# Up panels of a gated FFN in pairs with seven-product units, and convolution taps on ScalarE

## The chip, the cores and the metric

The kernel runs on one core of one Trainium2 chip. The metric is device time in microseconds (us). The profile is one execution of the program, taken by the hardware profiler. PE is TensorE (matmuls), PEld its weight loads, DVE is VectorE, ACT is ScalarE, POOL is GpSimd, SP is SyncE; the q behind an engine's name is its queue for DMA issues.

## The reference

A decoder trunk of two layers on 256 tokens with a width of 2048, all in float32: a gated linear attention layer (GLA), then a forgetting attention layer (FoX), each with a cross attention into 256 memory tokens and a channel mixer, which is what the change touches. Each mixer (here: FFN) is a gated MLP with a causal convolution of width 3 along the tokens between the up projection and the gate. In short:

```
a, val = split(rmsnorm(x) @ w_up)                      # two halves of 5632 columns
a   = a[t]*g2 + a[t-1]*g1 + a[t-2]*g0 + bias            # each column has its own g and bias
val = val[t]*g2 + val[t-1]*g1 + val[t-2]*g0 + bias
x   = x + (silu(a) * val) @ w_down
```

## The kernel before, in words

**Products.** All matmuls of the projections run on float32 split in a high and a low part. A weight unit is a tile [128, 1024] of 512 KB (two chunks of 128 rows of the contraction, 512 columns each). It is loaded by SP into a ring of five (`raw`), cast by ACT to its high part (`whi`, ring of four, line 210), and DVE subtracts to get the low part (`wlo`, ring of four, line 219). Three matmuls then make one product of a token block of 128 with one chunk: x high by w high (L231), x low by w high (L232), x high by w low (L235). For two token blocks and two chunks that is 12 matmuls of 128x512 a unit.

**The FFN.** The hidden width of 5632 is 44 chunks of 128, in three parts: chunks 0 to 15, 16 to 31, 32 to 43 (`PARTS`). For each part the up panels run first, then the down projection of these chunks, which adds to the residual x. An up panel makes two chunks of both halves a and val, 512 columns in all, from 8 units; parts 1, 2 and 3 have 8, 8 and 6 panels. The very first two panels of a layer run interleaved (`proj_two`), all others one by one (`proj_tm`).

**After a panel.** ACT evacuates each token block with the norm's scale (L1118), DVE transposes 32x32 blocks (L440), ACT's DMA queue writes the tile to DRAM (`turned`, L443) and reads it back in four pieces (L448), so that features lie on partitions and tokens along the free axis (`u`, two tiles in turn, two zero columns ahead). The convolution follows in two steps of one chunk each (`taken`): per chunk and half one ACT Identity with bias and scale (L1094) and two DVE scalar_tensor_tensor (L1095, L1096); then Silu on ACT (L1098), the product on DVE (L1099) and a split in high and low part (L525 on ACT, L526 on DVE) as the input of the down projection.

**Order.** `later(units, step)` puts a step behind the cast of that many units after the panel's end: write at 3, reads at 6, the two convolution steps at 8 and 9. Casts and low halves are placed ahead of their use with a priority. Each engine runs its own list in order, so an instruction that waits holds back all that stand behind it on that engine.

**Seven products.** In the down projection of parts 1 and 2 two output panels run as a pair (`proj_seven`). For chosen units (3 and 5, or 3, 5 and 7) a 2x2 block product of (two token blocks) by (two panels, two chunks) is made from seven instead of eight products, 21 matmuls in place of 24. It needs sums of the activations (`token_sums`, the `forms` tiles), and sums of the two raw weight tiles on DVE (t13 and t24, L348 to L351, four subtractions of 128x512), whose high and low parts are then made as usual (L316, L317, the single one as vhi and vlo). Extra accumulators m1, m5, m6 and m7 lie in the banks ps_t, ps_o and ps_s. A variant, `seven_evacuated`, sums these four into three SBUF tiles (L382 to L386) and adds the result at the evacuation with a DVE scalar_tensor_tensor (L483 in its one place so far, in the FoX layer's projections).

Of the kernel before, what the change touches and what calls it, by code (L numbers as in the profile page):

```python
# [31 lines left out]
PARTS = ((0, 16), (16, 32), (32, 44))  # L32
# [5 lines left out]
NUNIT = 1024  # L38
AHEAD = 300
SEVEN = ((3, 5), (3, 5, 7))  # L40
LAST = ()

SPREAD = [128 * q + 32 * k + i for k in range(4) for i in range(32) for q in range(4)]

# [95 lines left out]
def _trunk(ctx: ExitStack, tc: tile.TileContext, xt, xtok, memt, wp, wgu, gns, gfin, cnv, par, msk, out):  # L140
    nc = tc.nc
    where, _ = _layout()
# [37 lines left out]
    def later(*steps):  # L180

        for units, step in steps:
            due.append([units, step])
# [72 lines left out]
    def proj_two(keys, src, evacs, late):  # L256

        units = [where[k] for k in keys]
        base = min(min(u[1]) for u in units[0])
        acc = [[pacc.tile([P, 512], F32, name="acc", tag="acc") for _ in range(2)] for _ in keys]  # L260
        count = len(units[0])
        for part in (range(count - late), range(count - late, count)):
            for i in range(2):
                for u in part:
                    unit = units[i][u]
                    hi, lo = split_unit(unit)
                    products(list(enumerate(acc[i])), src, base, unit, hi, lo, u == 0, u == count - 1)
# [106 lines left out]
    def seven_evacuated(keys, src, forms, evacs, tiles):  # L374

        n = where[keys[0]][0][2]
        extra = {}

        def more(m1, m5, m6, m7):
            u, v, w = (tiles(t, F32)[:, :n] for t in ("s16", "s165", "s1675"))  # L380
            m1, m5, m6, m7 = (m[:, :n] for m in (m1, m5, m6, m7))
            S.activation(u, m1, AF.Copy)  # L382
            V.tensor_tensor(u, u, m6, ALU.add)
            V.tensor_tensor(v, u, m5, ALU.add)
            V.tensor_tensor(u, u, m7, ALU.add)
            V.tensor_tensor(w, u, m5, ALU.add)  # L386
            extra.update({(0, 0): m1, (1, 0): v, (0, 1): u, (1, 1): w})

        def evac(i):
            return lambda b, a: evacs[i](b, a, extra[i, b])  # L390

        proj_seven(keys, src, forms, [evac(i) for i in range(2)], tiles, more, True)

    def sums_of(src, chunks, f, h, form):
# [56 lines left out]
    def back():  # L451
        return tp.tile([P, 4, T], F32, name="back", tag="back", bufs=2)
# [65 lines left out]
    def split(dst, i, src, g=None, dealt=True):  # L518

        hi, lo = dst[i][:, 0, :], dst[i][:, 1, :]  # L520
        if dealt:
            hi, lo = (v.rearrange("p (h t) -> p h t", h=2) for v in (hi, lo))
            src = src.rearrange("p (t h) -> p h t", h=2)
        if g is None:
            S.activation(hi, src, AF.Copy)  # L525
            V.tensor_tensor(lo, src, hi.bitcast(F32), ALU.subtract)  # L526
        else:
            S.activation(hi, src, AF.Copy, scale=g)
            V.scalar_tensor_tensor(lo, src, g, hi.bitcast(F32), ALU.mult, ALU.subtract)  # L529
# [535 lines left out]
    def ffn(l, nx, h, m, then, ending=None):  # L1065
        with tc.tile_pool(name=f"ffn{l}", bufs=1) as fp, ExitStack() as ends:
            if ending:
                then = ending[0](ends)
            sums = ends.enter_context(ExitStack())
            sp = sums.enter_context(tc.tile_pool(name=f"sums{l}", bufs=1))  # L1070
            cw = fp.tile([P, 4 * 88], F32, name="cw")
            nc.sync.dma_start(cw, cnv[l])
            us = [fp.tile([P, 4, T + 2], F32, name=f"u{i}") for i in range(2)]
            for u in us:
                nc.gpsimd.memset(u[:, :, :2], 0.0)
            turn = [0]
            tiles = [sp.tile([P, 2, 4, P], F32R, name=f"forms{i}") for i in range(3)]
            held = []

            def spare_tile(name, dtype):  # L1080
                return sp.tile([P, 512 if name in ("vhi", "vlo") else NUNIT], dtype, name=name, tag=name)

            def form(t):
                return lambda i: [t[:, h, i, :] for h in range(2)]

            def taken(j, base, u, i):

                cv = []
                for c in range(2):
                    v = u[:, 2 * c + i, :]  # L1090
                    col = (c * 44 + j + i) * 4
                    w = [cw[:, col + n : col + n + 1] for n in range(4)]
                    r = fp.tile([P, T], F32, name=f"cv{c}", tag=f"cv{c}", bufs=3)
                    S.activation(r, v[:, 2:], AF.Identity, bias=w[3], scale=w[2])  # L1094
                    V.scalar_tensor_tensor(r, v[:, 1 : T + 1], w[1], r, ALU.mult, ALU.add)  # L1095
                    V.scalar_tensor_tensor(r, v[:, :T], w[0], r, ALU.mult, ALU.add)  # L1096
                    cv.append(r)
                S.activation(cv[0], cv[0], AF.Silu)  # L1098
                V.tensor_tensor(cv[1], cv[0], cv[1], ALU.mult)  # L1099
                split(m, j + i - base, cv[1])  # L1100
                if (j - base) // 2 in parts[base]:
                    held.append(cv[1])
                    if i:
                        summed(parts[base][(j - base) // 2])

            def summed(form):
                ab = [natural(h)[:, :, b] for h in held for b in range(2)]
                held.clear()
                token_sums(*ab, sp.tile([P, 4, P], F32, name="sf", tag="sf"), [form[:, h, :, :] for h in range(2)])

            def panel(j, base, slack=0):
                held = []

                def evac(b, a):
                    if not held:
                        held.append(Turn("turned"))
                    e = tp.tile([P, 512], F32, name="scaled", tag="scaled", bufs=2)
                    S.activation(e, a, AF.Copy, scale=nx.col()[:, b : b + 1])  # L1118
                    held[0].put(b, e)
                    if not b:  # L1120
                        return
                    u = us[turn[0] % 2]
                    turn[0] += 1
                    later((3, held[0].write), (6, lambda: held[0].read(lambda k: u[:, k, 2:])),
                          (8 + slack, lambda: taken(j, base, u, 0)), (9 + slack, lambda: taken(j, base, u, 1)))

                return evac

            parts = {lo: dict(zip(SEVEN[1] if p < len(PARTS) - 1 else LAST, tiles)) for p, (lo, _) in enumerate(PARTS)}
            for p, (lo, hi) in enumerate(PARTS):  # L1130
                forms = parts[lo]
                js = list(range(lo, hi, 2))
                if not p:
                    proj_two([("up", l, j) for j in js[:2]], h, [panel(js[0], lo), panel(js[1], lo, 2)], 2)
                    js = js[2:]
# [177 lines left out]
```

## Time and profile before

| what | value |
|---|---|
| median of 3 runs | 2239.39 us (2239.23 to 2240.11) |
| the profiled execution | 2239.32 us |
| its span, first to last instruction | 2237.6 us |
| mean granted TensorE clock | 0.999 |
| PE busy | 2225.4 us, 99% of the span |
| DVE busy | 1654.5 us, 74% |
| ACT busy | 1293.9 us, 58% |
| mean DMA rate | 231 GB/s |

Busy time leaves out register, branch, semaphore and DMA-issuing instructions. Durations of matmuls are latencies: they overlap, so a matmul's price is the time of a stretch divided by its count. Rows of the groups have line, engine, operation, output and input names, shapes, count, then busy us and mean ns, then idle time of the engine ahead of them and what ended it. The first layer's FFN spans 466.8 to 1179.2 us (up panels of the second part 725 to 899.2, its down panels to 983.2), the second layer's from 1515.5 us.

### The profile page before, as it was taken

The page shows a single profiled execution, that of the slowest core. Times are in us where ns is not written, and L with a number is a line of the kernel's source. Part 1 is how long each engine was busy: PE and PEld are TensorE (multiplying, and loading weights), DVE is VectorE, ACT ScalarE, POOL GpSimd, SP SyncE. Part 2 cuts the span into 40 slices and gives each one's busy share as a digit, 9 for nine tenths or more (in the row PEclk, how much of TensorE's full clock was granted, in tenths as well). Part 3 has the DMA queues.
Part 4 walks back from the last instruction along what each step waited for, and adds up shares of the span by engine and source line. Part 5 has one row for each costly group of instructions (what it writes and reads, how often), then busy time and mean ns, then how long its engine had stood idle before and what let it go on. Part 6 is the DMA issues. An engine that isn't in the chain of part 4 may idle for free.

```text
span 2237.6 us, 29679 instructions
## 1 busy us (share of the span) xinstructions
PE 2225.4 (99%) x10267; PEld 1862.4 (83%) x10267; DVE 1654.5 (74%) x2608; ACT 1293.9 (58%) x1921; POOL 44.7 (2%) x71
## 2 busy tenths in 40 slices
PE   9999999999999999999999999999999999999998
PEld 7888888888888888888888898888888888888886
DVE  8568987667689676886767875666778867797766
ACT  7555666556565565555656555455656556555554
POOL 0000000000000000000000000000000000000000
PEclk9999999999999999999999999999999999999999
DMA  9875667678766777667778777677877678766774
GB/s 340 277 233 188 211 201 227 192 251 247 244 226 207 236 236 242 216 209 242 232 255 276 236 231 229 196 236 246 249 240 235 199 235 243 236 214 217 237 236 140
DMA packets 276894, 516.98 MB, mean 231 GB/s; under 512 B 149884, under 2 KB 158600, under 8 KB 276616
## 3 DMA queue, kind: packets, MB, share of 16 engines
q1 hardware_dynamic: 124296, 427.24, 58.9%
q10 hardware_dynamic: 149760, 80.51, 12.5%
q0 software_dynamic: 2688, 7.34, 1.1%
q8 instruction: 80, 1.31, 0.2%
q14 instruction: 70, 0.57, 0.1%
HBM read 470.44 MB, written 44.58 MB: 230 GB/s over the span
## 4 chain that ended last, share of the span: by engine, by line
PE 99%; DMA 1%; DVE 0%; ACT 0%; SPq 0%; issue 0%; DVEq 0%; ACTq 0%
PE acc L232 26%; PE acc L231 26%; PE acc L235 26%; PE acc L293 16%; PE ps_s L293 1%; PE ps_o L293 1%; PE ps_t L293 1%; DMA back<-turned 0%; PE ps_s L835 0%; PE ps_t L625 0%; PE ps_s L636 0%; PE ps_o L647 0%; DMA raw<-wp 0%; PE ps_s L1008 0%; PE ps_o L855 0%; PE ps_o L1024 0%
## 5 line engine op out<-in xcount | busy, mean ns | idle before, releaser
L219 DVE TENSOR_TENSOR wlo<-raw,whi 128x1024 fp32r<-128x1024 f32 (+4 forms) x763 | 908.7, 1198 | 434.0 <-ACT whi L210 407.4
L210 ACT ACTIVATE whi<-raw 128x1024 fp32r<-128x1024 f32 (+4 forms) x763 | 785.4, 1038 | 622.6 <-PE acc L232 295.3
L231 PE MATMUL acc<-whi,B 128*128 128x512 f32 (+3 forms) x1440 | 548.3, 383 | 0.0
L232 PE MATMUL acc<-whi,B 128*128 128x512 f32 (+3 forms) x1440 | 547.9, 382 | 0.0
L231 PE MATMUL acc<-whi,A 128*128 128x512 f32 x1120 | 435.9, 392 | 0.7 <-ACT whi L210 0.5
L232 PE MATMUL acc<-whi,A 128*128 128x512 f32 x1120 | 435.0, 390 | 0.0
L235 PE MATMUL acc<-wlo,B 128*128 128x512 f32 (+3 forms) x1440 | 376.2, 381 | 0.0
L231 PEld LDWEIGHTS acc<-whi,B 128*128 128x128 f32 x1440 | 270.4, 188 | 46.7
L232 PEld LDWEIGHTS acc<-whi,B 128*128 128x128 f32 x1440 | 270.1, 188 | 46.3
L235 PEld LDWEIGHTS acc<-wlo,B 128*128 128x128 f32 x1440 | 267.9, 188 | 46.1
L235 PE MATMUL acc<-wlo,A 128*128 128x512 f32 x1120 | 301.5, 390 | 0.0
L231 PEld LDWEIGHTS acc<-whi,A 128*128 128x128 f32 x1120 | 210.3, 188 | 45.2 <-ACT whi L210 1.1
L232 PEld LDWEIGHTS acc<-whi,A 128*128 128x128 f32 x1120 | 210.3, 188 | 43.6 <-DVE A L529 0.2
L235 PEld LDWEIGHTS acc<-wlo,A 128*128 128x128 f32 x1120 | 210.2, 188 | 43.8 <-DVE wlo L219 0.3
L293 PE MATMUL acc<-whi,B 128*128 128x512 f32 x508 | 132.8, 390 | 0.0
L293 PE MATMUL acc<-whi,A 128*128 128x512 f32 x496 | 130.7, 390 | 0.0
L1094 ACT ACTIVATE cv<-u,cw 128x256 f32<-128x256 f32 x176 | 99.7, 593 | 40.9 <-DMA u<-turned 40.7
L293 PEld LDWEIGHTS acc<-whi,B 128*128 128x128 f32 x508 | 95.2, 188 | 19.9
L293 PEld LDWEIGHTS acc<-whi,A 128*128 128x128 f32 x496 | 93.2, 188 | 19.7
L1095 DVE SCALAR_TENSOR_TENSOR cv<-u,cw,cv 128x256 f32<-128x256 f32 x176 | 79.9, 480 | 18.7 <-ACT cv L1094 18.5
L440 DVE STREAM_TRANSPOSE square<-scaled 128x512 f32<-128x512 f32 x122 | 80.0, 690 | 0.0
L1096 DVE SCALAR_TENSOR_TENSOR cv<-u,cw,cv 128x256 f32<-128x256 f32 x176 | 77.7, 479 | 0.0
(260 smaller groups left out, 1797.3 us busy)
## 6 DMA issues: line engine op xcount, KB each, us to landing
raw<-wp SPq DMA_DIRECT2D x743, 512.0 KB, 4.4
turned<-square ACTq DMA_DIRECT2D x61, 512.0 KB, 5.1
u<-turned ACTq DMA_DIRECT2D x176, 128.0 KB, 4.2
raw<-wp SPq DMA_DIRECT2D x32, 384.0 KB, 3.3
raw<-wp SPq DMA_DIRECT2D x24, 388.0 KB, 4.6
xturned<-square ACTq DMA_DIRECT2D x12, 512.0 KB, 4.3
back<-xturned ACTq DMA_DIRECT2D x40, 128.0 KB, 4.3
raw<-wp SPq DMA_DIRECT2D x8, 400.0 KB, 3.5
```

The source lines that it names most:

```text
L210: casts.append(S.activation(hi[:, s], raw[:, s], AF.Copy))
L219: V.tensor_tensor(lo[:, s], raw[:, s], hi[:, s].bitcast(F32), ALU.subtract)
L231: TE.matmul(acc[:, :n], xh, hi[:, s], start=first and j == 0, stop=False)
L232: TE.matmul(acc[:, :n], xl, hi[:, s], start=False, stop=False)
L235: TE.matmul(a, xh, ls, start=False, stop=stop)
L293: TE.matmul(a[:, :n], x, w, start=k not in begun, stop=calls[k] == 0)
L440: V.transpose(self.square[:, :, :, b], src.rearrange("p (c t) -> p c t", t=32))
L1094: S.activation(r, v[:, 2:], AF.Identity, bias=w[3], scale=w[2])
L1095: V.scalar_tensor_tensor(r, v[:, 1 : T + 1], w[1], r, ALU.mult, ALU.add)
L1096: V.scalar_tensor_tensor(r, v[:, :T], w[0], r, ALU.mult, ALU.add)
```

## The change

Panels of a part now run in pairs through `seven_evacuated` as long as more than two panels are left in the part, and units 3 and 5 of each pair (`UP`) use seven products. Part 1 keeps its first `proj_two`, then has two pairs, part 2 has three pairs, part 3 two: seven a layer, 14 in all. The last two panels of each part stay in `proj_tm`. The sums of the FFN's input for units 3 and 5 (`mixed`) are made once per layer, 18 and 20 casts after its start.

The evacuation takes an extra operand: after ACT's scaled copy, DVE adds the scaled sum. The four sums at a pair's end now reuse the weight sum tiles t13 and t24, of which there is one each.

The convolution of all panels except the last of each part takes a new form, in four steps placed at 8, 9, 10 and 11 (10 to 13 for a pair's second panel): four ACT Identity taps with bias (`middle`), then twice four ACT Copy taps with a column scale and one DVE addition of 128x1024 (`side`), then one Silu and one product of 512 columns and two splits (`gated`). It uses the two `back` tiles. The last panel of each part keeps the old operations, in two steps of one chunk (`block`).

```diff
+UP = (3, 5)
...
-            u, v, w = (tiles(t, F32)[:, :n] for t in ("s16", "s165", "s1675"))
+            p, q = (tiles(t, F32) for t in ("t13", "t24"))
+            u, v, w = p[:, :n], p[:, n : 2 * n], q[:, :n]
...
+            def taps(t, u, j, n, c):
+
+                for i in range(2):
+                    k = 2 * c + i
+                    col = (c * 44 + j + i) * 4
+                    g = [cw[:, col + q : col + q + 1] for q in range(4)]
+                    if n == 2:
+                        S.activation(t[:, k, :], u[:, k, 2:], AF.Identity, bias=g[3], scale=g[2])
+                    else:
+                        S.activation(t[:, k, :], u[:, k, n : T + n], AF.Copy, scale=g[n])
...
+                def side(n):
+                    for c in range(2):
+                        taps(got[1], u, j, n, c)
+                    V.tensor_tensor(got[0], got[0], got[1], ALU.add)
...
+                def gated():
+                    a = got[0]
+                    S.activation(a[:, :2, :], a[:, :2, :], AF.Silu)
+                    V.tensor_tensor(a[:, 2:, :], a[:, :2, :], a[:, 2:, :], ALU.mult)
+                    for i in range(2):
+                        parted(i)
...
+                steps = [lambda i=i: block(i) for i in range(2)] if last else [
+                    middle, lambda: side(1), lambda: side(0), gated]
+                later(*[(at + i, step) for i, step in enumerate(steps)])
...
-                def evac(b, a):
+                def evac(b, a, extra=None):
...
+                    if extra is not None:
+                        V.scalar_tensor_tensor(e, extra, nx.col()[:, b : b + 1], e, ALU.mult, ALU.add)
...
+                while len(js) > 2:
+                    seven_evacuated([("up", l, j) for j in js[:2]], h, {u: form(t) for u, t in zip(UP, mixed)},
+                                    [panel(js[0], lo), panel(js[1], lo, 2)], spare_tile)
```

The order shows what moves. First PE, in the second part of the first layer. Before, a unit of one panel (chunks 6 and 7 of the FFN's input, B_106 and B_107):

```order
L231 MATMUL acc<-whi,B_106 128x512
L232 MATMUL acc<-whi,B_106 128x512
L231 MATMUL acc<-whi,B_107 128x512
L232 MATMUL acc<-whi,B_107 128x512
L231 MATMUL acc<-whi,B_106 128x512
L232 MATMUL acc<-whi,B_106 128x512
L231 MATMUL acc<-whi,B_107 128x512
L232 MATMUL acc<-whi,B_107 128x512
L235 MATMUL acc<-wlo,B_106 128x512
L235 MATMUL acc<-wlo,B_107 128x512
L235 MATMUL acc<-wlo,B_106 128x512
L235 MATMUL acc<-wlo,B_107 128x512
```

These twelve stand there once for each panel. The same chunks now, for two panels at once (line numbers of the changed kernel; ps_t is m1, ps_s are m5 and m7, mixed_4590 the sums of the input):

```order
L294 MATMUL ps_t<-whi,B_106 128x512
L294 MATMUL acc<-whi,B_107 128x512
L294 MATMUL ps_t<-whi,B_106 128x512
L294 MATMUL acc<-whi,B_107 128x512
L294 MATMUL ps_t<-wlo,B_106 128x512
L294 MATMUL acc<-wlo,B_107 128x512
L294 MATMUL acc<-vhi,mixed_4590 128x512 x2
L294 MATMUL acc<-vlo,mixed_4590 128x512
L294 MATMUL ps_s<-whi,mixed_4590 128x512 x4
L294 MATMUL ps_s<-wlo,mixed_4590 128x512 x2
```

With the six into ps_o and acc that follow, 21 matmuls stand in the place of 24, and they use four casts (v0, the half v1, t13, t24) of which two depend on DVE's sums.

Second ACT, from the write of the panel with chunks 20 and 21 (outputs A_88 and A_89) to its first taps. Before:

```order
L443 DMA turned<-square 128x1024
L210 ACTIVATE whi<-raw 128x1024
L448 DMA u_4583<-turned 128x4x64 x3
L210 ACTIVATE whi<-raw 128x1024
L448 DMA u_4583<-turned 128x4x64
L210 ACTIVATE whi<-raw 128x1024
L1094 ACTIVATE cv_7452<-u_4583,cw 128x256
L1094 ACTIVATE cv_7456<-u_4583,cw 128x256
L210 ACTIVATE whi<-raw 128x1024
```

The same place now, where the third pair of the second part runs beside it (L445 is the write, L450 a read, L1107 the taps with bias, L1109 the Copy taps, t_7746 and t_7747 the weight sums t13 and t24):

```order
L445 DMA turned<-square 128x1024
L317 ACTIVATE whi<-raw 128x1024
L450 DMA u_4583<-turned 128x4x64 x4
L1107 ACTIVATE back<-u_4583,cw 128x256 x2
L445 DMA turned<-square 128x1024
L317 ACTIVATE whi<-t_7746 128x1024
L1107 ACTIVATE back<-u_4583,cw 128x256 x2
L317 ACTIVATE whi<-t_7747 128x1024
L1109 ACTIVATE back<-u_4583,cw 128x256 x4
L211 ACTIVATE whi<-raw 128x1024
```

The reads and taps now stand closer to the write, with the casts of the weight sums behind and between the taps and the second panel's write among them.

Third ACT in the plain tail of the same part, at the panel with outputs A_92 and A_93, for one cast after another. Now:

```order
L450 DMA u_4583<-turned 128x4x64
L1107 ACTIVATE back<-u_4583,cw 128x256
L1109 ACTIVATE back<-u_4583,cw 128x256
L1107 ACTIVATE back<-u_4583,cw 128x256
L1109 ACTIVATE back<-u_4583,cw 128x256
L211 ACTIVATE whi<-raw 128x1024
L1107 ACTIVATE back<-u_4583,cw 128x256
L1109 ACTIVATE back<-u_4583,cw 128x256
L445 DMA turned<-square 128x1024
L1107 ACTIVATE back<-u_4583,cw 128x256
L1109 ACTIVATE back<-u_4583,cw 128x256
L211 ACTIVATE whi<-raw 128x1024
```

Four taps stand between two casts where two stood before.

More of the change, by code (lines that the diff above doesn't have):

```diff
@@ L1080, in spare_tile @@
             def spare_tile(name, dtype):
-                return sp.tile([P, 512 if name in ("vhi", "vlo") else NUNIT], dtype, name=name, tag=name)
+                return sp.tile([P, NUNIT if name in ("t13", "t24") else 512], dtype, name=name, tag=name)
             def form(t):
[L1084 to L1090, printed above, removed]
-                    col = (c * 44 + j + i) * 4
[L1092 to L1104, printed above, removed]
@@ new lines, in form, with mixed_at, step @@
+                return lambda i: [t[:, k, i, :] for k in range(2)]
+            mixed = [sp.tile([P, 2, 4, P], F32R, name=f"mixed{i}") for i in range(len(UP))]
+            def mixed_at(u, t):
+                def step():
+                    f, g = (tp.tile([P, 512], F32, name=n, tag="scaled", bufs=2) for n in ("sf", "sh"))
+                    sums_of(h, (2 * u, 2 * u + 1), f.rearrange("p (i t) -> p i t", t=P),
+                            g.rearrange("p (c t) -> p c t", t=T), [t[:, k, :, :] for k in range(2)])
+                return step
@@ new lines, in ffn @@
+            later(*[(18 + 2 * i, mixed_at(u, t)) for i, (u, t) in enumerate(zip(UP, mixed))])
+            def taps(t, u, j, n, c):
+                for i in range(2):
+                    k = 2 * c + i
+                    col = (c * 44 + j + i) * 4
+                    g = [cw[:, col + q : col + q + 1] for q in range(4)]
[3 more added lines that the diff above has]
+                        S.activation(t[:, k, :], u[:, k, n : T + n], AF.Copy, scale=g[n])
@@ new lines, in convolved, with tiles_of, middle, parted @@
+            def convolved(j, base, u, at, last):
+                got = []
+                def tiles_of(n):
+                    if not got:
+                        got.extend(back() for _ in range(n))
+                    return got
+                def middle():
+                    for c in range(2):
+                        taps(tiles_of(2)[0], u, j, 2, c)
+                def side(n):
+                    for c in range(2):
+                        taps(got[1], u, j, n, c)
+                    V.tensor_tensor(got[0], got[0], got[1], ALU.add)
+                def parted(i):
+                    split(m, j + i - base, got[0][:, 2 + i, :])
+                    c = (j - base) // 2
+                    if i and c in parts[base]:
+                        held.extend(got[0][:, 2 + n, :] for n in range(2))
+                        summed(parts[base][c])
+                def gated():
[4 more added lines that the diff above has]
+                        parted(i)
+                def block(i):
+                    a = tiles_of(1)[0]
+                    for c in range(2):
+                        k, col = 2 * c + i, (c * 44 + j + i) * 4
+                        g = [cw[:, col + q : col + q + 1] for q in range(4)]
+                        r = a[:, k, :]
+                        S.activation(r, u[:, k, 2:], AF.Identity, bias=g[3], scale=g[2])
+                        for n in (1, 0):
+                            V.scalar_tensor_tensor(r, u[:, k, n : T + n], g[n], r, ALU.mult, ALU.add)
+                    S.activation(a[:, i, :], a[:, i, :], AF.Silu)
+                    V.tensor_tensor(a[:, 2 + i, :], a[:, i, :], a[:, 2 + i, :], ALU.mult)
+                    parted(i)
+                steps = [lambda i=i: block(i) for i in range(2)] if last else [
+                    middle, lambda: side(1), lambda: side(0), gated]
+                later(*[(at + i, step) for i, step in enumerate(steps)])
@@ L1123, in evac @@
                     turn[0] += 1
-                    later((3, held[0].write), (6, lambda: held[0].read(lambda k: u[:, k, 2:])),
-                          (8 + slack, lambda: taken(j, base, u, 0)), (9 + slack, lambda: taken(j, base, u, 1)))
+                    later((3, held[0].write), (6, lambda: held[0].read(lambda k: u[:, k, 2:])))
+                    convolved(j, base, u, 8 + slack, j + 2 in (p[1] for p in PARTS))
                 return evac
@@ L1134, in ffn @@
                     proj_two([("up", l, j) for j in js[:2]], h, [panel(js[0], lo), panel(js[1], lo, 2)], 2)
+                    js = js[2:]
+                while len(js) > 2:
+                    seven_evacuated([("up", l, j) for j in js[:2]], h, {u: form(t) for u, t in zip(UP, mixed)},
+                                    [panel(js[0], lo), panel(js[1], lo, 2)], spare_tile)
                     js = js[2:]
```

## The prediction

> **What bounds the kernel now.** I read the page first, then the busy times by stage, the groups with shapes kept apart in one stage, and the timelines of DVE and ACT.
>
> ```profile
> span 2237.6 us, 29679 instructions
> ...
> PE 2225.4 (99%) x10267; PEld 1862.4 (83%) x10267; DVE 1654.5 (74%) x2608; ACT 1293.9 (58%) x1921; POOL 44.7 (2%) x71
> ...
> PE 99%; DMA 1%; DVE 0%; ACT 0%; SPq 0%; issue 0%; DVEq 0%; ACTq 0%
> ```
>
> PE is busy for 99% of the span, and the chain that ended last runs over PE alone. Fewer matmuls shorten the kernel, so long as PE is still fed. The averages of DVE (74%) and ACT (58%) hide the stages. These rows give the first FFN's second part, its up panels and then its down panels, and an older stage that already runs a pair with seven products and evacuates it the same way (start and end, length, then busy time of each engine, clock, DMA share, GB/s):
>
> ```profile
> 725.00:899.20 174.20, 174.20 (x770) 144.31 (x769) 124.29 (x181) 100.78 (x138) 0.00 (x0) 1.00 0.76 236
> 899.20:983.20 84.00, 84.00 (x370) 69.21 (x369) 74.26 (x97) 46.59 (x55) 0.00 (x0) 1.00 0.63 212
> 1241.00:1303.90 62.90, 62.90 (x278) 51.85 (x277) 53.01 (x68) 35.96 (x43) 2.99 (x4) 1.00 0.75 238
> ```
>
> In all three PE is busy from end to end at a granted clock of 1.00. In the down stage DVE is at 74.26/84.00 = 88% and PE still never waits. So 88% on DVE is covered; anything above is not shown.
>
> The groups of the up stage (725 to 899.2 us), shapes apart:
>
> ```profile
> L231 PE MATMUL acc<-whi,B 128*128 128x512 f32 x256 | 99.7, 389 | 0.0
> L232 PE MATMUL acc<-whi,B 128*128 128x512 f32 x256 | 99.6, 389 | 0.0
> ...
> L235 PE MATMUL acc<-wlo,B 128*128 128x512 f32 x256 | 68.6, 389 | 0.0
> ```
>
> The 389 ns is a latency and not a price: 768 matmuls filled 174.2 us, so one costs 174.2/768 = 0.227 us.
>
> **The change, part by part.** *Matmuls.* In each of the 14 pairs two units, each of 24 matmuls over both panels, go to 21. That is 14 x 2 x 3 = 84 matmuls, 84 x 0.227 = **19.1 us less** on PE. No other PE work is added. A pair goes from 192 x 0.227 = 43.6 us to 186 x 0.227 = 42.2 us. That is the time in which DVE and ACT must now do more.
>
> *DVE in a pair.* On DVE and ACT an instruction begins before the one ahead has ended, so I price from start to start. Back-to-back DVE rows (start, duration):
>
> ```profile
> 661.90 0.47 DVE L1095 SCALAR_TENSOR_TENSOR cv<-u,cw,cv 128x256 f32<-128x256 f32 x1
> 662.29 0.47 DVE L1096 SCALAR_TENSOR_TENSOR cv<-u,cw,cv 128x256 f32<-128x256 f32 x1
> ...
> 670.50 0.42 DVE L1099 TENSOR_TENSOR cv<-cv,cv 128x256 f32<-128x256 f32 x1
> 670.83 1.22 DVE L219 TENSOR_TENSOR wlo<-raw,whi 128x1024 fp32r<-128x1024 f32 x1
> ```
>
> ```profile
> 1260.81 0.74 DVE L483 SCALAR_TENSOR_TENSOR scaled<-s,ny,scaled 128x512 f32<-128x512 f32 x1
> 1261.47 0.70 DVE L440 STREAM_TRANSPOSE square<-scaled 128x512 f32<-128x512 f32 x1
> 1262.10 1.18 DVE L219 TENSOR_TENSOR wlo<-raw,whi 128x1024 fp32r<-128x1024 f32 x1
> ...
> 1287.59 0.69 DVE L350 TENSOR_TENSOR t<-raw,t 128x512 f32<-128x512 f32 x1
> 1288.19 1.22 DVE L317 TENSOR_TENSOR wlo<-raw,whi 128x1024 fp32r<-128x1024 f32 x1
> 1289.32 0.69 DVE L351 TENSOR_TENSOR t<-raw,t 128x512 f32<-128x512 f32 x1
> ```
>
> So a tap with add on 256 columns costs 0.39, a product of 256 columns 0.33, a scaled add of 512 columns 0.66, a transpose 0.63, an add of 512 columns 0.60, one of 1024 columns 1.13 us. Before, a pair costs 16 low halves x 1.13 + 4 transposes x 0.63 + two convolutions x (8 x 0.39 + 4 x 0.33) = 18.1 + 2.5 + 8.9 = 29.5 us. Four such pairs make 118, and the stage's row has 124 with the token sums and the end of the stage before. After: 12 plain low halves, 13.6; two seven-product units x (4 sums and one half-width low part x 0.60 + 3 low halves x 1.13 = 6.4), 12.8; the four sums at the end, 2.4; four scaled adds at the evacuation, 2.6; four transposes, 2.5; two convolutions x (2 adds of 1024 at 1.13 + a product of 512 at 0.60 + 2 low parts of 256 at 0.33 = 3.5), 7.1. Sum 41.0 us of 42.2, **97%**, where 88% is the most that the trace shows covered.
>
> *ACT in a pair.* ACT rows of the older seven-product stage, and of a convolution:
>
> ```profile
> 1245.67 1.07 ACT L210 ACTIVATE whi<-raw 128x1024 fp32r<-128x1024 f32 x1 [0.54 <-PE ps_t L293]
> 1246.64 0.57 ACT L382 ACTIVATE s<-ps_t 128x512 f32<-128x512 f32 x1
> 1247.12 1.05 ACT L210 ACTIVATE whi<-raw 128x1024 fp32r<-128x1024 f32 x1
> 1248.07 0.93 ACT L528 ACTIVATE A<-back,gains 128x256 fp32r<-128x256 f32 x2
> ```
>
> ```profile
> 783.38 1.08 ACT L1094 ACTIVATE cv<-u,cw 128x256 f32<-128x256 f32 x2
> ```
>
> A cast of 1024 columns takes 0.96 from start to start, a copy of 512 0.48. Two Copies of 256 columns with a column scale take 0.93 together, the second to its end; less the overlap that the cast shows (1.06 - 0.96 = 0.10) one is 0.41. Likewise a tap with bias and scale is (1.08 - 0.10)/2 = 0.49. The scaled evacuation and the split come from the groups of the up stage again (0.67 and 0.44, less the overlap 0.57 and about 0.35):
>
> ```profile
> L1118 ACT ACTIVATE scaled<-acc,ny 128x512 f32<-128x512 f32 x14 | 8.7, 674 | 0.0
> L525 ACT ACTIVATE A<-cv 128x256 fp32r<-128x256 f32 x14 | 6.2, 441 | 9.4 <-DVE cv L1099 9.4
> ```
>
> The new convolution has 4 taps with bias, 8 Copies, a Silu of 512 (as a copy, 0.5) and two splits: 4 x 0.49 + 8 x 0.41 + 0.5 + 2 x 0.35 = **6.4 us** of ACT a panel. A pair now has 18 casts of 1024 and 2 of 512 (18.3), one copy of 512 (0.5), four scaled evacuations (4 x 0.57 = 2.3) and two convolutions (12.8): 33.9 us, against 100.78/4 = 25.2 before. ACT also issues the DMAs of the turn through DRAM, which does not count as busy:
>
> ```profile
> 771.46 0.34 ACTq L443 DMA_DIRECT2D turned<-square  x1
> ...
> 776.38 1.48 ACTq L448 DMA_DIRECT2D u<-turned  x3
> 777.98 1.06 ACT L210 ACTIVATE whi<-raw 128x1024 fp32r<-128x1024 f32 x1 [3.59 <-issue]
> ...
> 780.89 0.60 ACT L1094 ACTIVATE cv<-u,cw 128x256 f32<-128x256 f32 x1 [0.90 <-DMA u<-turned]
> ```
>
> A write at 0.34 and four reads at 0.49 make 2.3 a panel, 4.6 a pair: 38.5 of 42.2 us, **91%**. The same rows show the real danger. The first read waits for the write to land (776.38 - 771.46 = 4.9 us), and the first tap for the read (4.5 us from 776.38). All the while ACT's later casts are queued behind; here the next cast stood idle 3.59 us. PE lost nothing, because ACT runs ahead:
>
> ```profile
> ACT whi L210 <- PE acc L232: 24.1, 20, 1.7
> ...
> ACT whi L210 <- issue: 13.4, 4, 4.1
> ```
>
> (total us, times, longest). Waits on PE for a free slot are the larger part, so the four-slot ring of casts was mostly full. Three slots ahead of the one in use are 3 x 12 x 0.227 = 8.2 us of cover. What stands in ACT's queue between write, read and taps decides.
>
> *The pairs one by one.* The first pair of parts 2 and 3 (numbered from 1) follows a down stage with no convolution beside its seven-product units: no stall by my walk. In the middle pair of part 2, in the second pair of part 3 and in the first pair of part 1 there are casts between write and reads and again between reads and taps: none either, with only 0.15 us to spare. In the second pair of part 1 and the third of part 2 just one cast stands between write and reads, and none between reads and taps, and the casts of the two weight sums queue behind these taps. From the write: reads at 4.9, first tap at 9.4, two taps, cast, two taps, cast: 9.4 + 4 x 0.49 + 2 x 0.96 = 13.3 us until the second sum is cast. PE has 8.2 us in the ring and (6 + 3 + 6) x 0.227 = 3.4 of the unit itself, 11.6 in all: 1.7 us late if every step waits for the one ahead. But a read's issue runs beside a cast (in the rows above the cast at 777.98 began while the reads were being issued). Walked cast by cast with that overlap I get 0.45 us for the first of the two pairs and 0.85 for the other.
>
> *The plain tail.* The last two panels of a part have PE at its old speed (16 x 12 x 0.227 = 43.6 us), but ACT convolves the pair's second panel and these in the new form. In part 2 I count between the 16 casts (15.4): 8 taps with bias (3.9), 20 Copies (8.2), 6 evacuations (3.4), 2 Silu (1.0), 4 splits (1.4), one cast of token sums (0.6), 3 writes and 11 reads (6.4): 40.3 us. Landings not covered by work in between add 2.4 + 1.5 (first panel), 1.5 and 0.9: 46.6, 3.0 us over. Full cover would make it 0, none and slow landings about 5.5. I take 3.0 for part 2, 1.0 for part 1, where more cover is left, 0 for part 3, whose down stage is of the old form with ACT light.
>
> *Price of the unseen.* Two mixed sums an FFN (a few half-microsecond steps on DVE and ACT in the first proj_two pair) lie under PE, with DVE at 71% in such a stage (124.29 of 174.20); I take 0, at most 2 x 0.7 us if that cover were gone. The single buffers of t13/t24 that the four last sums now reuse: 0; at worst the next pair's first sums wait for 2.4 us, six plain casts after the pair's end, so they don't.
>
> *Sum* on the profiled execution (2239.32 us, span 2237.6, so 1.7 lies outside): 2239.32 - 19.1 + 2 x (0.45 + 0.85 + 1.0 + 3.0) = 2239.32 - 19.1 + 10.6 = **2230.8 us**. The median of the runs, 2239.39, is the same within 0.1.
>
> **A rule against it.** By rows of this trace a tap is 0.39 on DVE and 0.41 to 0.49 on ACT, so moving 8 of them lengthens ACT by 3.2 us a panel and shortens DVE by only 0.9. The old taps would put DVE at 41.0 + 2 x 0.9 = 42.8 of 42.2 us, over the edge, 14 x 0.6 = 8.4 us of stalls. Then ACT would have cover and DVE none: 2239.3 - 19.1 + 8.4 = 2228.6, beside 2230.8 here. The choice of engine is worth 2 us either way, and I leave the sum as it is. The Trainium skill, page "ScalarE: Activation LUTs", section "Rules for kernel authors", says to put multiplies and adds on VectorE and not on ScalarE; the trace agrees on the price of one tap, but by that rule ACT and not DVE would be the engine at risk, which is the second rival below.
>
> **The rivals.** *All of it is covered*: the ring hides every landing, 2239.32 - 19.1 = 2220.2 us. For it: no PE wait in any FFN stage so far. Against: DVE 97%, ACT's sums in the tail. Chance 0.19. *ACT binds, slower*: ACT's 38.5 us a pair plus the uncovered landings of one panel (4.9 + 4.5, less the reads' own 2.0 and two casts of 0.96: 5.5) is 44.0, 1.8 over 42.2. It decides once the ring is not full again when a pair starts, so that the lead is gone for good. In the five pairs a layer with convolutions beside them that is 10 x 1.8 = 18 us, which eats the gain, and tails of 3.0 in two parts of each layer add 12: 2239.3 - 19.1 + 30 = 2250 us. For it: four waits of ACT behind landings in one stage already, of up to 4.1 us. Against: without landings ACT is at 91%. Chance 0.17. *No change*: stalls between 14.6 and 23.6 us (DVE's 97% alone, one late wlo of 1 us per pair, adds 14 to the 10.6, 2245 at most; half of it 2238). Chance 0.21. That the matmuls would not go is excluded by the order: PE loses them. *The forecast's own case*, stalls of 6 to 14.6 us, 2226 to 2234.8: 0.43.
>
> **How the numbers follow.** A measurement of this kernel tells 0.2%, 4.5 us, from no change: faster below 2234.9, slower above 2243.9. Faster is 0.43 + 0.19 = 0.62, same 0.21, slower 0.17. The range runs from full cover (2220.2, less 0.7 for the scatter of the runs before: 2219.5) into the slower case, to 2247, where about 0.12 is left above.
>
> **What would show it.** Right: fewer matmuls at 0.227 us, PE idle rows in front of L294 and L231 groups only in the second pair of part 1, the third of part 2 and the tails, released by casts, with ACT idle ahead of them for "issue" or u<-turned. Wrong: PE waiting on low halves (wlo) throughout the pairs, so that DVE binds; idle in the first pairs of parts 2 and 3; or no PE idle at all.

## The result, and the profile after

| | before | after |
|---|---|---|
| median of 12 runs each | 2239.36 us (2238.24 to 2240.22) | 2233.59 us (2229.12 to 2237.43) |
| ratio, 95% interval | | 0.9972 (0.9964 to 0.9980) |
| profiled execution | 2239.32 us, span 2237.6 | 2234.48 us, span 2232.7 |

The change makes the kernel 5.8 us faster by the medians; 8.5 us were forecast, and 19.1 us of matmuls went. The runs now lie 8.3 us apart where they lay 2.0 apart, and the places named below are those of the one profiled execution.

The page of the changed kernel, in the rows shown of before:

```profile
span 2232.7 us, 29804 instructions
...
PE 2214.0 (99%) x10183; PEld 1846.8 (83%) x10183; DVE 1808.7 (81%) x2650; ACT 1448.6 (65%) x2261; POOL 44.7 (2%) x71
...
PE 92%; DVE 2%; ACT 2%; DMA 2%; issue 1%; ACTq 0%; SPq 0%; DVEq 0%
```

PE has 84 matmuls less (10267 to 10183). But the chain that ended last is no longer PE alone: 8% of it now runs over DVE, ACT, DMA and issue. That share is no loss by itself: PE's own idle time went from 2237.6 - 2225.4 = 12.2 us to 2232.7 - 2214.0 = 18.7 us. Something holds PE a few times, and the view of what PE's matmuls waited for names it (total us, times, longest):

```profile
PE acc L294 <- ACT whi L211: 5.0, 3, 2.1
PE acc L232 <- ACT whi L211: 1.5, 2, 1.3
PE ps_o L177 <- DVE B L174: 1.5, 1, 1.5
PE ps_o L294 <- ACT whi L317: 1.1, 1, 1.1
```

The third row is the kernel's start and stands in both. The rest are late casts. They lie in a few places, and three causes show.

**A cast behind vhi, which waits for its weight tile.** The timeline of part 2, first layer, where the second pair gives way to the third. Counted back from the first matmul of the plain tail (853.82 us), 186 matmuls a pair, PE begins the third pair at 807.34 us:

```profile
808.94 0.33 SPq L325 DMA_DIRECT2D raw<-wp  x1
...
813.55 0.63 ACT L317 ACTIVATE vhi<-raw 128x512 fp32r<-128x512 f32 x1 [3.25 <-DMA raw<-wp]
...
814.09 1.04 ACT L211 ACTIVATE whi<-raw 128x1024 fp32r<-128x1024 f32 x1
...
815.18 4.11 PE L294 MATMUL acc<-whi,B 128*128 128x512 f32 x10 [2.10 <-ACT whi L211]
```

SP issued the load at 808.94, and it landed 4.6 us later. ACT stood 3.25 us at vhi, which belongs to a later unit of the third pair; the plain cast behind it was needed first, and PE idled 2.10 us. The second layer shows the same at 1858.9 (3.28 us at vhi, 1.91 us on PE), 6 us after its third pair began. On PE both losses lie in the third pair, and the rows of the pairs show it (second and third of the first layer):

```profile
764.85:807.34 42.49, 42.49 (x187) 34.71 (x186) 37.35 (x45) 33.02 (x53) 0.00 (x0) 1.00 0.71 230
807.34:853.82 46.48, 44.38 (x187) 36.13 (x187) 42.83 (x52) 35.40 (x56) 0.00 (x0) 0.96 0.75 236
```

(A count of 187 holds one matmul of the pair ahead.) The second pair takes 42.49 us, where the forecast priced 42.2 for the matmuls alone; the third takes 46.48.

**A cast behind reads that wait for their write.** The third pair of part 2, second layer:

```profile
1869.18 0.34 ACTq L445 DMA_DIRECT2D turned<-square  x1
...
1876.10 2.04 ACTq L450 DMA_DIRECT2D u<-turned  x4
...
1878.27 1.06 ACT L211 ACTIVATE whi<-raw 128x1024 fp32r<-128x1024 f32 x1 [3.10 <-issue]
...
1879.38 0.97 PE L294 MATMUL acc<-whi,A 128*128 128x512 f32 x3 [1.02 <-ACT whi L211]
```

The cast stands behind the reads, and the reads behind the write of 6.9 us earlier. This is the forecast's kind of wait, in the pair that it named, at another step: the forecast had the reads and taps of the first panel convolved there hold the casts of the weight sums, and here the second panel's reads hold a plain cast. Of the 3.10 us about 2 are the issuing of the four reads; the cast did not begin beside it. The end of part 3's tail, second layer, has such a place too: a write at 2163.80, its first read at 2169.09, the cast behind it at 2169.55, and 1.30 us of idle on PE.

**A cast of a weight sum behind the tail's convolution.** The start of the down stage of part 1, second layer:

```profile
1710.31 0.44 ACT L527 ACTIVATE B<-back 128x256 fp32r<-128x256 f32 x1 [3.28 <-DVE back L1153]
...
1712.12 0.68 DVE L352 TENSOR_TENSOR t<-raw,t 128x512 f32<-128x512 f32 x1
...
1712.92 1.06 ACT L317 ACTIVATE whi<-t 128x1024 fp32r<-128x1024 f32 x1 [1.79 <-DVE t L352]
...
1714.03 0.50 PE L294 MATMUL ps_o<-whi,forms 128*128 128x512 f32 x1 [1.10 <-ACT whi L317]
```

ACT waits for DVE's product, then for DVE's last weight sum, and PE for the cast of that sum.

I summed over all matmuls of 128x512 what each took from its start to the next start beyond 227 ns. Per place, in the FFN stages and in order of time: 2.3 + 1.7, 1.4, 2.2, 1.3, 0.4, 0.3 and 1.8 us, together 11.3 before rounding (the 1.7 are explained in the last section). A further 3.4 us more than before lies in excesses under 30 ns. So 2239.3 - 19.1 + 11.3 + 3.4 = 2234.9, which is the profiled run within 0.4 us.

Of the 3.4 us, 1.8 are in the 336 new matmuls that take the mixed input (14 pairs, two units, 12 each). Rows of the second pair of part 3, from start to start:

```profile
2094.70 1.07 PE L294 MATMUL acc<-wlo,A 128*128 128x512 f32 x4
...
2095.60 0.39 PE L294 MATMUL ps_t<-whi,A 128*128 128x512 f32 x1
...
2097.22 1.10 PE L294 MATMUL ps_s<-whi,mixed 128*128 128x512 f32 x4
...
2098.15 0.39 PE L294 MATMUL ps_t<-wlo,A 128*128 128x512 f32 x1
```

Four plain matmuls take 2095.60 - 2094.70 = 0.90 us, four with the mixed input 2098.15 - 2097.22 = 0.93 us: some 232 ns apiece in place of 226. The other 1.6 us are spread over some 8000 matmuls with plain input, about 0.2 ns each; what causes that is open.

### The profile page after: what moved, and what is told of

The parts are those of the page before. It is cut to its first block, busy times and chain, and to the rows that moved or that the text cites. A ratio compares the mean times of both kernels' runs of the same rounds, so it can differ in the third digit from the quotient of the medians.

```text
span 2232.7 us, 29804 instructions
## 1 busy us (share of the span) xinstructions
PE 2214.0 (99%) x10183; PEld 1846.8 (83%) x10183; DVE 1808.7 (81%) x2650; ACT 1448.6 (65%) x2261; POOL 44.7 (2%) x71
## 4 chain that ended last, share of the span: by engine, by line
PE 92%; DVE 2%; ACT 2%; DMA 2%; issue 1%; ACTq 0%; SPq 0%; DVEq 0%
PE acc L294 36%; PE acc L232 16%; PE acc L233 16%; PE acc L236 16%; PE ps_s L294 3%; PE ps_o L294 2%; PE ps_t L294 1%; DMA raw<-wp 1%; DMA turned<-square 1%; DVE wlo L220 1%; ACT whi L211 1%; ACT back L1109 1%; PE ps_s L837 0%; DVE wlo L318 0%; ACT back L1107 0%
## 5 line engine op out<-in xcount | busy, mean ns | idle before, releaser
L220 DVE TENSOR_TENSOR wlo<-raw,whi 128x1024 fp32r<-128x1024 f32 (+4 forms) x707 | 839.7, 1195 | 260.9 <-ACT whi L211 220.0
L232 PE MATMUL acc<-whi,B 128*128 128x512 f32 (+3 forms) x992 | 373.6, 381 | 1.3 <-ACT whi L211 1.3
L233 PE MATMUL acc<-whi,B 128*128 128x512 f32 (+3 forms) x992 | 373.3, 379 | 0.0
L294 PE MATMUL acc<-whi,B 128*128 128x512 f32 x1236 | 324.7, 392 | 2.1 <-ACT whi L211 2.1
L294 PE MATMUL acc<-whi,A 128*128 128x512 f32 x1224 | 321.6, 390 | 2.9 <-ACT whi L211 2.9
L232 PE MATMUL acc<-whi,A 128*128 128x512 f32 x672 | 261.3, 394 | 0.3 <-ACT whi L211 0.2
L233 PE MATMUL acc<-whi,A 128*128 128x512 f32 x672 | 260.3, 391 | 0.0
L236 PE MATMUL acc<-wlo,B 128*128 128x512 f32 (+3 forms) x992 | 257.0, 377 | 0.0
L236 PEld LDWEIGHTS acc<-wlo,B 128*128 128x128 f32 x992 | 183.7, 188 | 28.7
L294 PE MATMUL acc<-wlo,B 128*128 128x512 f32 x618 | 174.4, 390 | 0.0
L318 DVE TENSOR_TENSOR wlo<-t,whi 128x1024 fp32r<-128x1024 f32 x102 | 123.8, 1221 | 35.1 <-ACT whi L317 27.8
L317 ACT ACTIVATE whi<-t 128x1024 fp32r<-128x1024 f32 x102 | 106.8, 1054 | 66.3 <-PE acc L294 44.2
L236 PEld LDWEIGHTS acc<-wlo,A 128*128 128x128 f32 x672 | 126.0, 188 | 26.4 <-DVE wlo L220 0.3
```

Of the source, the lines that this page charges most:

```text
L220: V.tensor_tensor(lo[:, s], raw[:, s], hi[:, s].bitcast(F32), ALU.subtract)
L232: TE.matmul(acc[:, :n], xh, hi[:, s], start=first and j == 0, stop=False)
L233: TE.matmul(acc[:, :n], xl, hi[:, s], start=False, stop=False)
L236: TE.matmul(a, xh, ls, start=False, stop=stop)
L294: TE.matmul(a[:, :n], x, w, start=k not in begun, stop=calls[k] == 0)
L317: casts.append(S.activation(hi, raw, AF.Copy))
```

## The experiments

Medians, and ratios to the kernel before, which ran again on the same chip (2239.4 to 2239.7 us); the changed kernel itself has 2233.6 us. Each edit is made to the changed kernel, unless it says the kernel before. An edit that moves one instruction can also change the order of others in an engine's list.

**The convolution alone.**

```diff
-                while len(js) > 2:
+                while len(js) > 99:
```

> The new convolution alone, no panel pairs in the FFN; all matmuls as before. Theory A (what makes PE wait is the order of ACT's list, where casts stand behind a transfer that has not landed; sums of busy time do not): the ring of casts is full again after each landing, so PE idles at most now and then, 2239 to 2242 us. Rival B (the sums count: ACT at 40.3 us plus 6.3 us of landings in 43.6 us for two plain panels, as the forecast had it in the tail, 3.0 us over): about 19 double panels x 3.0 us more, 2290 us or above.

Measured: 2248.1 us, ratio 1.0041 (1.0028 to 1.0053). Neither: 8.4 us lost, more than theory A's 3 and far from B's 50. The profiled execution's PE waits lie at the starts of the down stages of parts 1 and 2, where the tail's convolution meets the weight sums:

```profile
1693.19 1.71 ACT L1109 ACTIVATE back<-u,cw 128x256 f32<-128x256 f32 x4 [0.34 <-DVE back L1127]
...
1694.80 1.04 ACT L211 ACTIVATE whi<-raw 128x1024 fp32r<-128x1024 f32 x1
1694.92 1.23 DVE L1127 TENSOR_TENSOR back<-back 128x1024 f32<-128x1024 f32 x1 [0.64 <-ACT back L1109]
1695.89 2.11 PE L294 MATMUL acc<-whi,B 128*128 128x512 f32 x8 [0.90 <-ACT whi L211]
```

Taps wait for the add and the add for the taps, and the cast stands behind them. In the middle of a part nothing was lost, so B's per-panel sum is wrong. The 8.4 us are near the forecast's tail term (2 x (1.0 + 3.0) = 8), but the places are not: from start to start the profiled execution loses 3.3 us at part 1 and 2.2 at part 2, where 2.0 and 6.0 were forecast, and four of these waits are for a late low half from DVE.

**The old taps with the pairs.**

```diff
-                steps = [lambda i=i: block(i) for i in range(2)] if last else [
+                steps = [lambda i=i: block(i) for i in range(2)] if True else [
```

> The 14 pairs with the old form of the convolution in every panel: ACT 3.1 us a panel lighter, DVE at 42.8 us of the 42.2 us that a pair has. Theory A: fewer ACT instructions between casts, vhi still waits for its weights, 2224 to 2231 us. Rival B (load sums): DVE is over the edge by 0.6 us in each of 14 pairs, 8 us of PE waits on low halves (wlo) over the pairs, and ACT's own waits gone: 2228 us with PE idle spread over all pairs, 2232 or more if DVE's late sums also hold back the casts of t13 and t24.

Measured: 2243.7 us, ratio 1.0015 (1.0006 to 1.0023). Slower than before, and 10 us slower than with the taps on ACT. Waits lie in the pairs, as B had it, but they are larger, and most of them are for casts, as the second half of B had it. The edit also has two steps a panel in place of four, so engine and placing change together. The third pair of part 2:

```profile
840.90 1.66 DVE L1151 SCALAR_TENSOR_TENSOR back<-u,cw,back 128x256 f32<-128x256 f32 x4
...
844.75 0.67 DVE L352 TENSOR_TENSOR t<-raw,t 128x512 f32<-128x512 f32 x1
...
845.46 1.06 ACT L317 ACTIVATE whi<-t 128x1024 fp32r<-128x1024 f32 x1 [0.82 <-DVE t L352]
...
846.57 0.55 PE L294 MATMUL ps_o<-whi,mixed 128*128 128x512 f32 x1 [1.86 <-ACT whi L317]
```

The last weight sum (L352) is queued behind taps on DVE, ACT waits for it to cast, and PE for the cast. DVE's fullness reaches PE through ACT.

**The reads on GpSimd's queue.**

```diff
-                    later((3, held[0].write), (6, lambda: held[0].read(lambda k: u[:, k, 2:])))
+                    later((3, held[0].write), (6, lambda: held[0].read(lambda k: u[:, k, 2:], queue=nc.gpsimd)))
```

> The four reads of each up panel's turn are issued from GpSimd's queue, so that no cast stands behind a read that waits for its write to land; the taps still wait for the read. Theory A: the events with a cast held by issue (1.3 us in the second layer's second part, 1.8 us at the end of its third part, in the profiled run after) are gone, those behind vhi (2.3 + 1.7 and 2.1 us) stay: 2229 to 2232 us. Rival B (ACT's and DVE's sums): ACT loses only 2.0 us of issuing a panel that ran beside casts anyway, 2233 us. A third case: reads on GpSimd land later and the taps hold the casts instead, 2235 us or more.

Measured: 2229.3 us, ratio 0.9952 (0.9939 to 0.9966); the runs lie within 2.4 us of each other again. That is theory A's time. Total and longest of ACT's "issue" waits go from 32.7 and 3.1 (after, first row) to 18.1 and 2.4 us (second):

```profile
ACT whi L211 <- issue: 32.7, 20, 3.1
```

```profile
ACT whi L211 <- issue: 18.1, 12, 2.4
```

But A's places are only half right: the 2 us waits on a plain cast behind vhi, which A let stay, are not in its profiled execution. PE waits there on evacuations that stand behind vhi (in the view of PE):

```profile
PE acc L294 <- ACT scaled L1172: 2.6, 4, 0.9
```

**vhi behind the cast of v0**, in every seven-product unit of the kernel, the old ones too:

```diff
-                v1 = halves(r1[:, n:], True)
+                with tc.issue_after(casts[-1].ins):
+                    v1 = halves(r1[:, n:], True)
```

> The cast and the low half of the single half tile (vhi, vlo) are put behind the cast of v0 in every seven-product unit of the kernel, so that no plain cast stands behind a vhi that waits for its weight tile. Theory A: the two events of the profiled run after at the end of the second pair of part 2 (2.3 us with 1.7 us of slow clock behind it, and 2.1 us) are gone, about 6 us: 2227 to 2230 us. Rival B: the raw tile is then freed later and the next loads come later, PE waits elsewhere, 2233 to 2236 us.

Measured: 2240.2 us, ratio 1.0008 (0.9999 to 1.0017): 6.6 us slower than the changed kernel. The edit moved the waits and made more of them (PE's waits):

```profile
PE ps_o L294 <- ACT whi L317: 4.5, 4, 1.4
PE acc L294 <- ACT whi L211: 4.5, 7, 1.2
```

**One seven-product unit a pair.**

```diff
-UP = (3, 5)
+UP = (3,)
```

> Only unit 3 of each of the 14 pairs in seven products, unit 5 plain: 42 matmuls less instead of 84, 9.5 us; DVE a pair 41.0 - 6.4 + 4 x 1.13 = 39.1 of 42.9 us (91%), ACT nearly as before the edit. Theory A (casts held behind landings, one event for each pair whatever the number of units): 2239.4 - 9.5 + some 8 = 2238 us, 2235 to 2240. Rival B (DVE at 97% is what costs): with 91% most waits go, 2239.4 - 9.5 + 3 = 2233 us, as fast as with both units.

Measured: 2250.1 us, ratio 1.0045 (1.0033 to 1.0058). Both theories fall: with DVE less loaded and 9.5 us of matmuls gone, 20 us are lost. The start of part 2's down stage shows the third cause again, which did not hold PE there in the changed kernel:

```profile
932.82 0.68 DVE L352 TENSOR_TENSOR t<-raw,t 128x512 f32<-128x512 f32 x1
...
933.62 1.06 ACT L317 ACTIVATE whi<-t 128x1024 fp32r<-128x1024 f32 x1 [1.78 <-DVE t L352]
```

PE waited 1.04 us there. Over the kernel the casts of the weight sums are its largest wait:

```profile
PE ps_o L294 <- ACT whi L317: 5.4, 6, 1.0
```

So neither the load nor the number of units sets the loss; the lists differ in many places. Which displacement does it was not isolated.

**Write and reads on GpSimd's queue.** (The write's queue is handed through as a parameter.)

```diff
-                    later((3, held[0].write), (6, lambda: held[0].read(lambda k: u[:, k, 2:])))
+                    later((3, lambda: held[0].write(nc.gpsimd)), (6, lambda: held[0].read(lambda k: u[:, k, 2:], queue=nc.gpsimd)))
```

> Write and reads of the up panels' turn both from GpSimd's queue, so that ACT issues none of them and waits neither for the transposes ahead of the write nor for its landing. Theory A: less held than with the reads alone, 2225 to 2229 us. Rival B (what is left, vhi's weights and DVE's 97%, has nothing to do with the turn): 2229 to 2230 us, as with the reads alone.

Measured: 2232.4 us, ratio 0.9972 (0.9961 to 0.9983). No better than the changed kernel, and 3 us behind the reads alone. Both theories expected less time. The write now shares a queue with reads that wait for writes; that this is the cause is argued, not shown. Its profiled execution (2235.5 us) has the two waits behind vhi again, 2.07 us of idle on PE at 816.8 and 1.97 at 1862.7.

**The convolution alone, reads on GpSimd's queue** (the edits of the first and the third experiment together).

> The new convolution alone (no pairs), reads on GpSimd's queue. It splits the 8.4 us that the convolution alone costs. Theory A (landings that hold casts): 2240 to 2243 us. Rival B (ACT's sum of work, and the taps' own chain of Copy, add, Copy on one tile at the end of a part): 2246 to 2249 us.

Measured: 2347.4 us, ratio 1.0486 (1.0472 to 1.0500). Neither: it is 108 us slower than the kernel before. The next one shows the same wait.

**The kernel before, reads on GpSimd's queue.**

```diff
-                    later((3, held[0].write), (6, lambda: held[0].read(lambda k: u[:, k, 2:])),
+                    later((3, held[0].write), (6, lambda: held[0].read(lambda k: u[:, k, 2:], queue=nc.gpsimd)),
```

> The kernel before with the reads of the up panels' turn on GpSimd's queue, as a control. PE does not wait in any FFN stage before, so both theories have 2239.4 us, within 1 us.

Measured: 2290.4 us, ratio 1.0225 (1.0211 to 1.0239). Both theories expected no change; 51 us were lost in a kernel whose FFN never waited. The end of part 1:

```profile
630.29 2.96 ACT L210 ACTIVATE whi<-raw 128x1024 fp32r<-128x1024 f32 x3 [1.00 <-DVE square L440]
...
635.71 2.96 POOL L448 DMA_DIRECT2D u<-turned  x4 [21.69 <-DMA turned<-square]
...
641.11 0.60 ACT L1094 ACTIVATE cv<-u,cw 128x256 f32<-128x256 f32 x1 [7.86 <-DMA u<-turned]
...
644.68 1.60 PE L293 MATMUL acc<-whi,A 128*128 128x512 f32 x5 [2.52 <-ACT whi L210]
```

Three casts stand between the write and the first tap, as mostly in the kernel before. There, though, the reads stood behind the first of them: ACT waited in two parts, at the reads and at the tap (3.59 and 0.90 us in the rows of the prediction), and two casts ran while the reads landed. Now all three casts run at once, and the tap then waits in one piece for what is left of the write's landing and then for its read, issued on GpSimd (2.96 us for the four reads), to land: 7.86 us, with the casts behind it. Over the kernel ACT's waits of this kind went from 40.7 us, at most 2.0 long (before, first row), to 276.8 us, up to 9.5 us long (second). The convolution alone with the same reads has them too (third):

```profile
ACT cv L1094 <- DMA u<-turned: 40.7, 59, 2.0
```

```profile
ACT cv L1094 <- DMA u<-turned: 276.8, 84, 9.5
```

```profile
ACT back L1107 <- DMA u<-turned: 243.3, 74, 8.7
```

In the changed kernel the same edit left this wait nearly as it was (42.5 us with the reads on ACT's queue, 45.7 on GpSimd's).

So a wait moves to wherever the next instruction that needs the data stands, and a place that does well in one list does harm in the other.

**vhi behind the evacuations.** A list records each scaled evacuation of an up panel, and vhi and vlo follow the last one:

```diff
-                v1 = halves(r1[:, n:], True)
+                with tc.issue_after((evacs_done or casts)[-1].ins):
+                    v1 = halves(r1[:, n:], True)
```

> One thing moved: each vhi and vlo stands behind the last scaled evacuation issued so far, so that at a pair's end the casts and evacuations come first and vhi, which waits for its weight tile, after them. Theory A (order of the list): the two events of the profiled run after at the end of the second pair of part 2 (2.3 us with 1.7 us of slow clock, and 2.1 us) go, 6 us: 2228 to 2230 us. Rival B: the half tile then comes late for the unit, or the raw slot is freed late, as when vhi stood behind v0 (2240 us): 2233 us or more.

Measured: 2233.5 us, ratio 0.9971 (0.9961 to 0.9981), the same as the changed kernel. In its profiled execution (2229.2 us, the fastest of its eight) the two events behind vhi are gone, but the median did not move: in time it is rival B. So it is not shown that these two events cost the median anything. What the slower executions wait for was not profiled; PE's largest wait in this one, after the kernel's start:

```profile
PE ps_o L294 <- ACT whi L317: 1.9, 3, 1.0
```

**Both, vhi behind the evacuations and the reads on GpSimd's queue.**

> The same move of vhi, and the four reads from GpSimd's queue. Theory A: the four PE waits of about 1 us on an evacuation that stood behind vhi go as well, 2229.3 - 4 = 2225 us, 2224 to 2227. Rival B: 2229 us, as with the reads alone.

Measured: 2229.3 us, ratio 0.9953 (0.9941 to 0.9966), as with the reads alone: rival B. The four waits on evacuations are gone from the profiled execution, the fastest of its five at 2225.7 us; two runs stand at 2232.2.

**Three slots in the ring of high parts**, in the changed kernel and, as the control, in the kernel before:

```diff
-RING = {"raw": 5, "whi": 4, "wlo": 4}
+RING = {"raw": 5, "whi": 3, "wlo": 4}
```

> The changed kernel with three slots instead of four in the ring of high parts (whi): the cover is 2 x 2.72 = 5.4 us instead of 8.2. Theory A (waits of ACT of 3 to 5 us in the queue, covered by the ring): many of them now reach PE, 2245 us or more. Rival B (busy sums at 91% to 97% of a pair are the limit): a slot less changes little, 2234 to 2238 us.

> Control: the kernel before with three slots in the ring of high parts. Its longest waits of ACT behind a landing are 4 to 5 us and it has less work in the lists. Theory A: 2240 to 2244 us, a small part of what the changed kernel loses. Rival B: 2239.4 us.

Measured: 2261.0 us, ratio 1.0105 (1.0084 to 1.0125), and for the kernel before 2241.0 us, ratio 1.0007 (0.9998 to 1.0016). The edit costs the changed kernel 27 us and the one before 1.6 us, which is not clear of noise. PE's longest wait on a cast is 5.0 us in the one (first row) and 1.5 in the other:

```profile
PE ps_o L294 <- ACT whi L317: 10.9, 5, 5.0
```

```profile
PE acc L231 <- ACT whi L210: 2.6, 4, 1.5
```

The longest wait, in the third pair of part 2, has the cast of a weight sum behind the four reads, and the sum itself late:

```profile
833.14 2.32 ACTq L450 DMA_DIRECT2D u<-turned  x4
...
835.58 1.06 ACT L317 ACTIVATE whi<-t 128x1024 fp32r<-128x1024 f32 x1 [4.67 <-DVE t L350]
...
836.69 0.79 PE L294 MATMUL ps_o<-whi,mixed 128*128 128x512 f32 x1 [4.95 <-ACT whi L317]
```

This is the clearest result: the changed kernel lives on the lead of its casts and the kernel before hardly does. Busy sums, which the edit leaves alone, do not give the 27 us. The edit is not pure, though: it reorders ACT's list in both kernels (by their rows, at most 1964 of 2248 computing instructions keep their order in the changed one, 1718 of 1908 in the other), so how much of the 27 us is the slot and how much the order is not separated.

## Why the prediction was right, and where it was not

- *84 matmuls less, 19.1 us.* The count was right, the price of the others was not. I gave every matmul 0.227 us; those with mixed input take some 232 ns, and 1.8 us of the gain stayed there, with 1.6 us more spread over the plain ones. The kernel before ran matmuls with such sums in its down stages, and I didn't price them apart.
- *DVE and ACT in a pair.* The prices held: a Copy tap lasts 495 ns, which is some 0.40 us once the overlap of 0.10 is taken off, for 0.41 priced. In the 42 us around the turn from part 2's second to its third pair (784 to 826 us) DVE is busy for 39.29 us, 94%, a stall included. By pair it is busy for 37.35 of 42.49 us in the second and 42.83 of 46.48 in the third, so the 97% was not reached in either, and that it would be covered is not shown. With the old taps, worked out at 42.8 us of 42.2, the pairs did wait.

```profile
L1109 ACT ACTIVATE back<-u,cw x304: 489/495/512, 518.1 to 2164.3; 128x256 f32<-128x256 f32 x152
```

```profile
784.00:826.00 42.00, 39.90 (x168) 32.13 (x167) 39.29 (x50) 32.01 (x52) 0.00 (x0) 0.96 0.75 236
```

- *The ring as cover.* Right in kind: with three slots the changed kernel loses 27 us and the one before 1.6. I forecast 10.6 us of stalls and the profiled execution has 11.3, of which 1.7 passed at a lower clock, for which I had no term.
- *The places.* Half right. The third pair of part 2 was named, and 7.4 of the 11.3 us lie there, over both layers, where I had 1.7. But 6.1 of them come from vhi behind its weight tile's load, which my walk does not have, and 1.3 from the second panel's reads in one layer; the wait for the first panel's reads, which the walk was about, cost PE nothing (ACT stood 4.13 us there at 1867.84). The second pair of part 1, priced at 0.9, lost next to nothing; the second of part 3, priced at 0, lost 0.4; of the tails part 1's lost 1.4 in one layer, part 2's none, and part 3's, priced at 0, 2.1. That the sum came out so near is luck in good part, and the median lies only 1.3 us below the border to "no change" (2234.9).
- *The tail.* In the changed kernel it was oversized. Where the convolution runs alone the median loses 8.4 us, near the 8 of the term, but part 1 loses more than part 2, against the forecast.
- *The rule against it.* I gave the choice of engine 2 us either way. With the taps on DVE, and the steps placed as before, it is worth 10: 2243.7 us. The 8.4 us of that branch were less than half the price; the rows show a late weight sum on DVE that also holds ACT and the casts behind it. The rule of the Trainium skill ("ScalarE: Activation LUTs", "Rules for kernel authors": adds and multiplies on VectorE) would have made this kernel slower than before, by 4 us, although the rows agree with it on one tap (0.39 us on VectorE, 0.41 to 0.49 on ScalarE).
- *The rivals.* Full cover did not come; the fastest run of 12 was 2229.1 us, against 2220.2. The slower case, a lead gone for good, did not come either with four slots. A time like it came with three (2261), but that the lead was gone for good there is not shown.

What stays open: why one seven-product unit a pair loses 20 us, why the runs lie 8 us apart, and what holds the median at 2229 once reads and vhi are moved.

## What to carry to other kernels

On an engine that works a list in order, an instruction that waits is paid for by whatever stands behind it; price the wait against the lead in the ring at that place and not against the engine's busy share. Taking a slot from the ring is a cheap test of how much lead is in use, if the old kernel gets the same edit as a control. When work is moved off such a list, look at what now waits in its place, and whether work still runs between two waits: the same edit gave 4 us in one kernel and cost 51 in the other.

## What the runs showed of the hardware

A PE wait can cost more than its length. After the 2.10 us of idle in the changed kernel the granted clock was 0.50 for about 3 us (clock is the third number from the end of a row):

```profile
812.50:815.20 2.70, 0.60 (x4) 0.18 (x2) 2.09 (x5) 1.65 (x3) 0.00 (x0) 0.99 0.75 246
815.20:818.20 3.00, 3.00 (x7) 2.42 (x8) 3.00 (x4) 2.02 (x3) 0.00 (x0) 0.50 0.52 202
```

The matmuls in these 3.0 us start some 427 ns apart, and 1.7 us more were lost. The 1.91 us of idle at 1858 us in the same execution had no such sequel. The Trainium skill, "TensorE: Matmul & The Clock Gate", section "Part 1: The HAM clock gate (the "warmup" mystery)", puts the fall to half rate after an idle window of about 3.4 us; here a gap of 2.1 us was enough. The length of a gap alone does not decide it: with vhi behind the cast of v0 a gap of 1.37 us (before 1979.9 us, with another of 0.75 us two us ahead of it) was followed by 3.4 us at 0.50, and in the kernel before with the reads on GpSimd's queue a gap of 2.60 us (before 1985.4 us) left the clock at 1.00.
